# Block products added onto sums in PSUM, the last weight sum made by accumulating transfers, and down rows taken in steps of two

## The chip, the cores and the metric

One Trainium2 chip, one of its cores. The metric is the device time of one execution in microseconds, as the median over several runs. The profile is one profiled execution of the same program; its page gives the span from the first to the last instruction.

## The reference, cut to what matters

Two layers, each of a SwiGLU block, a token mixer (short gated convolution, a gated linear recurrence, a pooling branch), a cross attention and a second SwiGLU block. Each of these four parts ends in a residual sum and a layer norm. Tokens are 256, the model width is 1024, the hidden width of a SwiGLU block is 2816, all in float32. The change touches the four SwiGLU blocks:

```
def swiglu(x, w_gate, w_up, w_down):
    return (jax.nn.silu(x @ w_gate) * (x @ w_up)) @ w_down
h = layer_norm(ALPHA * h + 0.5 * swiglu(h, ffn1_gate[l], ffn1_up[l], ffn1_down[l]), ...)
```

## The kernel before

**Numbers in two parts.** Each float32 operand is split into a rounded high part and the rest: `split` (L60) has ScalarE write the high part (L61) and VectorE subtract it (L62). `mm_rows` (L129) makes one product as three matmuls: high times high, high times low, low times high. `load` (L64) fetches weights through SyncE's queue into a ring of six `raw` tiles of 128x1024, and every one of them is split into a tile `whi` and a tile `wlo`, from rings of eight.

**A SwiGLU block** (`ffn`, L400) walks over the hidden width in chunks of 512, numbered c = 0 to 5, the last of 256. `first` makes chunk 0, `hidden` (L538) the ordinary chunks: all products of x with the gate columns into two PSUM banks (one for each half of the tokens), `activate` (L434) takes them through Silu into the tile `sg`, then all products with the up columns, `gated` (L438) multiplies, and `turn` (L446) brings the result into the layout that the down projection needs: four transfers deal `sg` over the partitions (L450), VectorE transposes 32x32 blocks (L453), and `split` makes `ah` and `al`. `both(c, u)` is one slab of the down projection: 24 matmuls that add chunk c's activations times 256 rows of down into the four `dn` banks (`ys`). Behind the products of chunk c stand `both(c-2, 1)` and `both(c-1, 0)`.

**Block-product chunks.** For c in `sevens` (L679: 2 and 4, in the first block of layer 0 only 4, so seven chunks in all) `by_seven` (L568) computes both gate and up of the chunk with seven products of half the depth (512) and one half of the tokens in place of eight. Blocks of weights (`w00`, `w10` of gate, `w01`, `w11` of up) lie in two tiles each and are summed in place by VectorE (`parts_of`, L593, the add is L597); the sums of blocks of x (`bx`) are made once for a SwiGLU block (`blocks_of_x`, L552) and kept in `kTh` and `kTl`. One product is `run` (L610): 4 depths times 3 matmuls, 12 in all. The seven results go to seven PSUM tiles, four and then three from a ring of four, and are put together by a ScalarE copy (L625) and seven VectorE additions (`put`, L618); `left` (L641) ends with two Silu (L648), two multiplications (L649) and `turn`.

**What sets the order.** The program is written in the order that the text shows, and a scheduling layer places the instructions of each engine; in a few stretches (the start, the recurrence) the order is given by hand. Each engine then runs its own list in order: an instruction that waits holds all that stand behind it on that engine. An instruction that writes into a ring's tile waits until the last reader of the tile before it is done.

**PSUM layout.** `product` (L102) writes column c + 256 h of the result to place 2c + h of the bank. `by_two` (L430) therefore reads a bank in two instructions, one for each parity, with 256 elements each.

Of the kernel before, what the change touches and what calls it, by code (L numbers as in the profile page):

```python
# [17 lines left out]
P = 128  # L18
# [28 lines left out]
def model(ctx: ExitStack, tc: tile.TileContext, t: dict, out: bass.AP):  # L47
# [13 lines left out]
        nc.scalar.copy(hi, src)  # L61
        lows.append(nc.vector.tensor_tensor(lo, src, hi.bitcast(F32), op=ALU.subtract))  # L62

    def load(src, k0, nk, c0, ncol, fine=False):  # L64


        hi, lo, todo = [], [], []
        step = 2048 // ncol
        for a in range(k0, k0 + nk, step):
            half = step // 2  # L70
            raw = [
                wp.tile([P, 1024], F32, tag="raw", name="raw", bufs=6).rearrange("p (k c) -> p k c", c=ncol)
                for _ in range(2)
            ]
            part = 1 if fine else half
            for b in range(0, step, part):
                loads.append(nc.sync.dma_start(
                    raw[b // half][:, b % half : b % half + part, :],
                    src[(a + b) * P : (a + b + part) * P, c0 : c0 + ncol].rearrange("(k p) c -> p k c", p=P),
                ))  # L80
# [12 lines left out]
        return Weights(hi, lo, half, todo)  # L93
# [5 lines left out]
            "p (h c) -> p h c" if len(a.shape) == 2 else "p r (h c) -> p r h c", h=2  # L99
        )  # L100

    def product(o, w, x, start, stop):  # L102
        x = x.rearrange("p (h c) -> p c h" if len(x.shape) == 2 else "p r (h c) -> p r c h", h=2)
        o = o.rearrange("p (c h) -> p c h" if len(o.shape) == 2 else "p r (c h) -> p r c h", h=2)
        nc.tensor.matmul(o, w, x, start=start, stop=stop)  # L105


    def sums(o):
# [17 lines left out]
        nc.vector.tensor_tensor(dst, o[:, 0], dst, op=ALU.add)  # L126


    def mm_rows(o, xh, xl, wh, wl, start, stop):  # L129
        product(o, xh, wh, start, False)  # L130
        product(o, xh, wl, False, False)
        product(o, xl, wh, False, stop)

    def tok(i):
        return slice(i * P, (i + 1) * P)
# [47 lines left out]
    def load_memory(mp, behind):  # L183
        m = [
            mp.tile([P, DM], F32, tag=f"spare{n}", name="m", bufs=1).rearrange("p (k b j) -> p k b j", k=4, j=32)
            for n in range(2)
        ]
        with tc.issue_after(behind.ins):
            for n in range(2):
                for a in range(4):  # L190
                    for k in range(4):
                        c = (4 * n + k) * P + a * 32
                        nc.gpsimd.dma_start(
                            m[n][a * 32 : a * 32 + 32, k],
                            t["mem"][0, :, c : c + 32].rearrange("(b i) j -> i b j", i=32),
                        )

        def later():
            for n in range(2):
                for k in range(0, 4, 2):  # L200
                    turned = mp.tile([P, 2, SEQ], F32, tag="up", name="turned")
                    nc.vector.transpose(
                        turned.rearrange("p k t -> p (k t)"), m[n][:, k : k + 2].rearrange("p k b j -> p (k b j)")
                    )
                    d = slice(4 * n + k, 4 * n + k + 2)
                    split(mTh[:, d, :], mTl[:, d, :], turned)

        return later

# [190 lines left out]
    def ffn(l, name, n, pend=None, last=False, early=None):  # L400
        gate, up, down = (t[f"{name}_{x}"][l] for x in ("gate", "up", "down"))
        with tc.tile_pool(name="ffn", bufs=2, reuse_waits="tile") as fp:
# [22 lines left out]


            def ordered(v):
                return v.rearrange("p (a k j) -> p k a j", a=4, j=32)

            def by_two(v, o):  # L430
                o = o.rearrange("p (n a j m) -> p m n a j", n=2, a=4, m=2)
                return [(ordered(v)[:, 2 * m : 2 * m + 2], o[:, m]) for m in range(2)]

            def activate(s, i, og):  # L434
                for v, o in by_two(s[:, i, :], og):
                    nc.scalar.activation(v, o, AF.Silu)

            def gated(s, i, ou):  # L438
                for v, o in by_two(s[:, i, :], ou):
                    nc.vector.tensor_tensor(v, o, v, op=ALU.mult)  # L440

# [4 lines left out]
            def turn(s):  # L446
                ah, al = act_tiles()
                x = fp.tile([P, 4, NT, P], F32, tag="dealt", name="dealt", bufs=1)
                for a in range(4):
                    nc.sync.dma_start(x[a * 32 : a * 32 + 32], s[:, :, a * P : (a + 1) * P])  # L450
                for i in range(NT):
                    d = fp.tile([P, 4, P], F32, tag="up", name="square")
                    nc.vector.transpose(  # L453
                        d.rearrange("p k (b r) -> p b k r", b=4), x[:, :, i, :].rearrange("p b (k j) -> p b k j", k=4)
                    )
                    split(ah[:, :, tok(i)], al[:, :, tok(i)], d)
                return ah, al

            def first():
# [105 lines left out]
                    split(*parts[n], q[o])  # L565
                return parts

            def by_seven(c0, bx):  # L568
                def rows_by_columns(r):
                    return r.rearrange("p (k c) -> p k c", c=CHUNK)  # L570

# [38 lines left out]
                def run(o, x, w):  # L610
                    for k in range(4):
                        wh, wl = w.at(k, slice(0, CHUNK))
                        mm_rows(o, x[0][:, k, :], x[1][:, k, :], wh, wl, k == 0, k == 3)

                def half_sum():
                    return fp.tile([P, 4, P], F32, tag="up", name="half").rearrange("p k t -> p (k t)")

                def put(o, a, op, b):  # L618
                    nc.vector.tensor_tensor(halves(o), sums(a), halves(b), op=op)

                s = activations()
                g = [s[:, i, :] for i in range(NT)]
                o = [acc((P, CHUNK)) for _ in range(4)]
                run(o[0], part_of_x(0, 0), parts_of(w00))
                nc.scalar.copy(halves(g[0]), sums(o[0]))  # L625
                run(o[2], bx[0], parts_of(w00, w01))
                run(o[1], bx[1], parts_of(w00, w11))
                e = half_sum()
                put(e, o[1], ALU.add, g[0])
                run(o[3], bx[2], parts_of(w01, w11))  # L630
                put(g[1], o[3], ALU.add, e)
                f = half_sum()
                put(f, o[2], ALU.subtract, g[1])
                put(e, o[2], ALU.subtract, e)
                o = [acc((P, CHUNK)) for _ in range(3)]
                run(o[0], bx[3], parts_of(w11))
                run(o[1], part_of_x(0, 1), parts_of(w10))
                run(o[2], part_of_x(1, 1), parts_of(w00, w10))


                def left():  # L641
                    put(e, o[0], ALU.add, e)
                    for i in range(NT):
                        put(g[i], o[1 + i], ALU.add, g[i])
                    s = fp.tile([P, NT, CHUNK], F32, tag="spare2", name="sg", bufs=1)
                    for i, u in enumerate((e, f)):
                        v = ordered(s[:, i, :])
                        nc.scalar.activation(v, g[i].rearrange("p (k a j) -> p k a j", a=4, j=32), AF.Silu)  # L648
                        nc.vector.tensor_tensor(v, v, u.rearrange("p (k a j) -> p k a j", a=4, j=32), op=ALU.mult)  # L649
                    return turn(s)  # L650

                return left
# [1 line left out]
            def last_hidden(c0):  # L654

                ah, al = act_tiles()
                s = activations()[:, 0, :].rearrange("p (j c) -> p j c", j=2)
                r = fp.tile([P, 2, SEQ], F32, tag="up", name="up")
# [12 lines left out]
                return ah, al  # L671

            def slab(c, u):
                w = load(down, c * 4 + 2 * u, 2, 0, DM)
                ah, al = acts[c]
                return w, ah[:, 2 * u : 2 * u + 2, :], al[:, 2 * u : 2 * u + 2, :]

# [34 lines left out]
            for c, (c0, ncol) in enumerate(chunks):  # L712
# [1 line left out]
                    acts.append(first())  # L714
                    ys = [[acc((P, 512), "dn") for _ in range(2)] for _ in range(NT)]
                elif c in sevens:
                    left = by_seven(c0, bx)
                else:
                    if c in (1, 2) and early is not None:
                        acts.append(hidden(c0, aside))  # L720
# [500 lines left out]
```

## Time and profile before

| what | value |
|---|---|
| median of 3 runs | 1071.56 us (1070.53 to 1072.04) |
| span of the profiled execution | 1068.8 us |
| TensorE busy, granted clock | 1059.3 us, 0.998 |
| VectorE busy | 946.3 us (89%) |
| ScalarE busy | 642.4 us (60%) |
| GpSimd busy | 66.4 us (6%) |
| DMA moved | 231.90 MB |

The page gives the span of the profiled execution (its own time within the kernel); the runs' times contain 2 to 3 us around it. "Busy" of TensorE is modelled: matmuls overlap, one begins before the one ahead has ended, so the distance from start to start is what counts. In rows of instruction groups the columns are line, engine, operation, output<-inputs, count | total us, mean ns of one | idle time just before them and what ended it. In rows of the timeline they are start, duration, engine, line, operation, tiles and count, and in brackets the idle time ahead and what ended it.

### The profile page before, as it was taken

Reading aid. Unit: us, or ns where it says so; the run is one execution under the profiler, and the core shown is the slowest. Engines: PE = TensorE matmul, PEld = TensorE weight load, DVE = VectorE, ACT = ScalarE, POOL = GpSimd, SP = SyncE. Lnnn points to the kernel's source line nnn. Section 1 sums busy time; section 2 is a strip of 40 time slices with the busy share of each in tenths; the row PEclk is TensorE's granted clock in tenths of the full one; section 3 lists DMA queues with packets and bytes.
Section 4 is the critical chain, followed back from the end, with each engine's and each line's share of the span. In section 5 each row is a group of like instructions: output and inputs, shape, how many; then the busy total and the mean of one; then the engine's idle time right before and its main releaser. Section 6 shows DMA issues by size and latency. Waiting matters only on the chain.

```text
span 1068.8 us, 16312 instructions
## 1 busy us (share of the span) xinstructions
PE 1059.3 (99%) x5966; PEld 937.7 (88%) x5966; DVE 946.3 (89%) x1318; ACT 642.4 (60%) x916; POOL 66.4 (6%) x114
## 2 busy tenths in 40 slices
PE   9999999999999999999999999999999999999997
PEld 7888888889899888888888888888898998888886
DVE  6977997998988799999799999788989787999996
ACT  7555664666557565656575557566764665656660
POOL 9700001000000000000000000010000000000000
PEclk9999999999999999999999999999999999999999
DMA  9997484755574575848675865856536665759461
GB/s 362 262 307 256 129 288 165 249 176 174 170 278 167 178 252 194 290 167 218 238 272 184 256 254 183 290 179 216 196 126 213 241 227 181 257 156 334 134 223 40
DMA packets 130895, 231.90 MB, mean 217 GB/s; under 512 B 9408, under 2 KB 48608, under 8 KB 130816
## 3 DMA queue, kind: packets, MB, share of 16 engines
q1 hardware_dynamic: 129024, 228.49, 64.8%
q0 software_dynamic: 1216, 1.20, 0.5%
q8 instruction: 47, 0.77, 0.3%
q10 hardware_dynamic: 576, 1.18, 0.3%
q14 instruction: 32, 0.26, 0.1%
HBM read 216.15 MB, written 1.05 MB: 203 GB/s over the span
## 4 chain that ended last, share of the span: by engine, by line
PE 99%; DMA 0%; DVE 0%; issue 0%; DVEq 0%
PE acc L105 65%; PE dn L105 31%; PE acc L172 1%; PE dn L923 1%; PE dn L982 0%; DMA h<-in_x_dram 0%; PE acc L491 0%; PE dn L981 0%; PE dn L971 0%; PE acc L1047 0%; PE dn L888 0%; DVE h L358 0%; DVE h L353 0%; PE dn L472 0%; DVE st L338 0%
## 5 line engine op out<-in xcount | busy, mean ns | idle before, releaser
L61 ACT CAST whi<-raw 128x1024 fp32r<-128x1024 f32 (+1 forms) x438 | 442.9, 1042 | 197.5 <-DVE raw L597 54.9
L62 DVE TENSOR_TENSOR wlo<-raw,whi 128x1024 fp32r<-128x1024 f32 (+1 forms) x438 | 515.7, 1209 | 32.6 <-ACT whi L61 29.0
L105 PE MATMUL acc<-whi,xT 128*128 128x512 f32 x1032 | 312.9, 380 | 0.0
L105 PEld LDWEIGHTS acc<-whi,xT 128*128 128x128 f32 x1032 | 195.1, 189 | 27.5
L105 PE MATMUL acc<-wlo,xT 128*128 128x512 f32 x516 | 195.6, 379 | 0.0
L105 PE MATMUL acc<-xT,whi 128*128 128x512 f32 x576 | 142.3, 383 | 0.2
L105 PE MATMUL dn<-whi,ah 128*128 128x512 f32 x346 | 131.5, 380 | 0.0
L105 PE MATMUL dn<-wlo,ah 128*128 128x512 f32 x346 | 131.2, 379 | 0.0
L105 PE MATMUL dn<-whi,al 128*128 128x512 f32 x346 | 131.2, 379 | 0.0
L105 PEld LDWEIGHTS acc<-xT,whi 128*128 128x128 f32 x576 | 104.0, 190 | 12.5 <-ACT whi L61 0.7
L105 PEld LDWEIGHTS acc<-wlo,xT 128*128 128x128 f32 x516 | 97.5, 189 | 13.8
L105 PE MATMUL dn<-whi,xT 128*128 128x512 f32 x288 | 87.9, 381 | 0.0
L105 PEld LDWEIGHTS acc<-xT,wlo 128*128 128x128 f32 x576 | 75.5, 191 | 3.9
L105 PE MATMUL acc<-xT,wlo 128*128 128x256 f32 x576 | 75.9, 275 | 0.0
L105 PEld LDWEIGHTS dn<-whi,al 128*128 128x128 f32 x346 | 65.4, 189 | 9.2
L105 PEld LDWEIGHTS dn<-wlo,ah 128*128 128x128 f32 x346 | 65.4, 189 | 9.2
L105 PEld LDWEIGHTS dn<-whi,ah 128*128 128x128 f32 x346 | 65.4, 189 | 9.1
L350 POOL TENSOR_TENSOR rs<-rs,nhalf 128x1 f32<-128x1 f32 x16 | 14.9, 930 | 833.6 <-DVE rs L346 598.1
L597 DVE TENSOR_TENSOR raw<-raw 128x1024 f32<-128x1024 f32 x56 | 66.2, 1217 | 0.4
L105 PEld LDWEIGHTS dn<-whi,xT 128*128 128x128 f32 x288 | 54.4, 189 | 7.7 <-DVE xT L62 0.3
L105 PE MATMUL dn<-wlo,xT 128*128 128x512 f32 x144 | 54.6, 379 | 0.0
L332 DVE SCALAR_TENSOR_TENSOR h<-h,dn 128x512 f32<-128x512 f32 x31 | 21.2, 683 | 32.9 <-PE dn L105 32.9
(234 smaller groups left out, 1277.5 us busy)
## 6 DMA issues: line engine op xcount, KB each, us to landing
raw<-in_ffn_up_dram SPq DMA_DIRECT2D x88, 512.0 KB, 5.3
raw<-in_ffn_down_dram SPq DMA_DIRECT2D x88, 512.0 KB, 6.6
raw<-in_ffn_gate_dram SPq DMA_DIRECT2D x84, 512.0 KB, 5.1
raw<-in_w_in_dram SPq DMA_DIRECT2D x48, 512.0 KB, 4.7
dealt<-sg SPq DMA_DIRECT2D x80, 128.0 KB, 4.7
raw<-in_ca_k_dram SPq DMA_DIRECT2D x16, 512.0 KB, 4.9
raw<-in_w_out_dram SPq DMA_DIRECT2D x16, 512.0 KB, 4.5
raw<-in_ca_v_dram SPq DMA_DIRECT2D x16, 512.0 KB, 5.3
```

The source lines that it names most:

```text
L61: nc.scalar.copy(hi, src)
L62: lows.append(nc.vector.tensor_tensor(lo, src, hi.bitcast(F32), op=ALU.subtract))
L105: nc.tensor.matmul(o, w, x, start=start, stop=stop)
L172: nc.tensor.transpose(pt[:, k, :], src[:, (4 * j + k) * P : (4 * j + k + 1) * P], unit)
L332: nc.vector.scalar_tensor_tensor(v, v, ALPHA / scale, sums(y[i][n]), op0=ALU.mult, op1=ALU.add, accum_out=None if junk is None else st[:, ...
L350: nc.gpsimd.tensor_tensor(rs, rs, nhalf[:, 0:1], op=ALU.pow)
L597: nc.vector.tensor_tensor(r[i], r[i], plus[i], op=ALU.add)
L923: nc.tensor.matmul(o[g, hh, :], kc[:, hh, g], x, start=True, stop=True)
```

## The change

1. **Three products onto closed sums** (`by_seven`). There are three PSUM tiles in place of seven, here A (`o[0]`), B (`o[1]`), C (`o[2]`). In the order of the text: P1 = x00·w00 into A; ScalarE copies A to `s[:,0]` (the s-copy); P2 = bx0·(w00+w01) into B; P3 = bx1·(w00+w11) added onto A; ScalarE copies A to `e` (the e-copy); P4 = x01·w10 into C; P5 = bx2·(w01+w11) added onto A; VectorE adds C to `s[:,0]`, ScalarE takes Silu of it and copies A to `f` (the f-copy); `both(c-2, 1)`; VectorE makes `f` = B - `f`; P6 = bx3·w11 added onto B; P7 = x11·(the last sum of w00) added onto A. Then `both(c-1, 0)` and `left`: Silu of A into `s[:,1]`, `e` = B - `e`, one multiplication of 128x1024, `turn`. TensorE must wait with P3 for the s-copy, with P5 for the e-copy, with P6 for `f`, with P7 for the f-copy.
2. **The last weight sum** is not made by VectorE from `w10`: two DMAs of 512 KB issued by GpSimd add the block of gate from HBM onto the two tiles of `w00` (`accum_op`), after VectorE has made the low parts of (w00+w11).
3. **Down rows in steps of two.** `load(..., dealt=True)` for the slabs of chunks 0 to 4 takes rows 2p + u in place of p; number of DMAs and bytes are the same (each row is 4 KB). The activations then lie in the bank's own order, and `activate` and `gated` read a bank with one instruction of 512 elements in place of two of 256 (`in_order`).
4. **One split in `turn`**: both halves of the tokens are transposed into one tile, and split by one ScalarE and one VectorE instruction of 128x1024 in place of two of 128x512 each. The tag `up` holds one buffer of 4 KB a partition in place of two of 2 KB; the transposed tiles, `e` and `f`, and `turned` of the memory's loading take turns in it.

The core of the diff:

```diff
-    def product(o, w, x, start, stop):
+    def product(o, w, x, start, stop, more=False):
...
-        nc.tensor.matmul(o, w, x, start=start, stop=stop)
+        nc.tensor.matmul(o, w, x, start=start, stop=stop, skip_group_check=more)
...
+                if dealt:
+                    c, u = divmod(a // 2, 2)
+                    at = slice(c * CHUNK + 2 * P * b, c * CHUNK + 2 * P * (b + 1))
+                    rows = src[at, c0 : c0 + ncol].rearrange("(p u) c -> p u c", u=2)[:, u, :]
+                    loads.append(nc.sync.dma_start(to[:, 0, :], rows))
...
             def activate(s, i, og):
-                for v, o in by_two(s[:, i, :], og):
-                    nc.scalar.activation(v, o, AF.Silu)
+                nc.scalar.activation(ordered(s[:, i, :]), in_order(og), AF.Silu)
...
+                d = fp.tile([P, NT, 4, P], F32, tag="up", name="square", bufs=1)
                 for i in range(NT):
-                    d = fp.tile([P, 4, P], F32, tag="up", name="square")
                     nc.vector.transpose(
...
-                    split(ah[:, :, tok(i)], al[:, :, tok(i)], d)
+                d = d.rearrange("p i k t -> p k i t")
+                split(*(y.rearrange("p k (i t) -> p k i t", i=NT) for y in (ah, al)), d)
...
-                o = [acc((P, CHUNK)) for _ in range(4)]
+                ef = fp.tile([P, NT, CHUNK], F32, tag="up", name="halves", bufs=1)
+                e, f = ef[:, 0, :], ef[:, 1, :]
+                def taken(o, bank):
+                    nc.scalar.copy(ordered(o), in_order(bank))
+                o = [acc((P, CHUNK)) for _ in range(2)]
                 run(o[0], part_of_x(0, 0), parts_of(w00))
-                nc.scalar.copy(halves(g[0]), sums(o[0]))
-                run(o[2], bx[0], parts_of(w00, w01))
-                run(o[1], bx[1], parts_of(w00, w11))
...
+                taken(s[:, 0, :], o[0])
+                run(o[1], bx[0], parts_of(w00, w01))
+                run(o[0], bx[1], parts_of(w00, w11), True)
+                for i in range(2):
+                    k = 4 + 2 * i
+                    nc.gpsimd.dma_start(
+                        w00[i], gate[k * P : (k + 2) * P, c0 : c0 + CHUNK].rearrange("(k p) c -> p k c", p=P),
+                        accum_op=ALU.add,
+                    )
+                taken(e, o[0])
+                o.append(acc((P, CHUNK)))
+                run(o[2], part_of_x(0, 1), parts_of(w10))
+                run(o[0], bx[2], parts_of(w01, w11), True)
+                put(s[:, 0, :], o[2], ALU.add, s[:, 0, :])
+                nc.scalar.activation(s[:, 0, :], s[:, 0, :], AF.Silu)
+                taken(f, o[0])
+                between()
+                put(f, o[1], ALU.subtract, f)
+                run(o[1], bx[3], parts_of(w11), True)
+                run(o[0], part_of_x(1, 1), parts_of(w00), True)
...
                 def left():
+                    activate(s, 1, o[0])
+                    put(e, o[1], ALU.subtract, e)
+                    nc.vector.tensor_tensor(s, s, ef, op=ALU.mult)
                     return turn(s)
...
-                    if c > 1:
+                    if c > 1 and c not in sevens:
                         both(c - 2, 1)
+                    if c < len(chunks) - 1:
+                        both(c - 1, 0)
                     if c in sevens:
                         acts.append(left())
-                    if c < len(chunks) - 1:
-                        both(c - 1, 0)
```

`between` is `both(c-2, 1)`; `run` with `more` true starts no new sum. The number of matmuls is the same.

More of the change, by code (lines that the diff above doesn't have):

```diff
@@ L62, in split, with load @@
         lows.append(nc.vector.tensor_tensor(lo, src, hi.bitcast(F32), op=ALU.subtract))
-    def load(src, k0, nk, c0, ncol, fine=False):
+    def load(src, k0, nk, c0, ncol, fine=False, dealt=False):
         hi, lo, todo = [], [], []
@@ L76, in load @@
             for b in range(0, step, part):
[L77 to L80, printed above, removed]
+                to = raw[b // half][:, b % half : b % half + part, :]
+                if dealt:
[3 more added lines that the diff above has]
+                    loads.append(nc.sync.dma_start(to[:, 0, :], rows))
+                else:
+                    loads.append(nc.sync.dma_start(
+                        to, src[(a + b) * P : (a + b + part) * P, c0 : c0 + ncol].rearrange("(k p) c -> p k c", p=P)
+                    ))
             for s in range(2):
@@ L126, in add, with mm_rows @@
         nc.vector.tensor_tensor(dst, o[:, 0], dst, op=ALU.add)
[L129 to L132, printed above, removed]
+    def mm_rows(o, xh, xl, wh, wl, start, stop, more=False):
+        product(o, xh, wh, start, False, more)
+        product(o, xh, wl, False, False, more)
+        product(o, xl, wh, False, stop, more)
     def tok(i):
@@ L200, in later @@
                 for k in range(0, 4, 2):
-                    turned = mp.tile([P, 2, SEQ], F32, tag="up", name="turned")
+                    turned = mp.tile([P, NT, CHUNK], F32, tag="up", name="turned", bufs=1)[:, 0, :]
                     nc.vector.transpose(
-                        turned.rearrange("p k t -> p (k t)"), m[n][:, k : k + 2].rearrange("p k b j -> p (k b j)")
+                        turned, m[n][:, k : k + 2].rearrange("p k b j -> p (k b j)")
                     )
                     d = slice(4 * n + k, 4 * n + k + 2)
-                    split(mTh[:, d, :], mTl[:, d, :], turned)
+                    split(mTh[:, d, :], mTl[:, d, :], turned.rearrange("p (k t) -> p k t", k=2))
         return later
@@ L427, in ordered, with in_order @@
             def ordered(v):
[L428 to L432, printed above, removed]
+                return v.rearrange("p (a k j) -> p a k j", a=4, j=32)
+            def in_order(o):
+                return o.rearrange("p (a j k) -> p a k j", a=4, j=32)
             def activate(s, i, og):
-                for v, o in by_two(s[:, i, :], og):
-                    nc.scalar.activation(v, o, AF.Silu)
+                nc.scalar.activation(ordered(s[:, i, :]), in_order(og), AF.Silu)
             def gated(s, i, ou):
-                for v, o in by_two(s[:, i, :], ou):
-                    nc.vector.tensor_tensor(v, o, v, op=ALU.mult)
+                v = ordered(s[:, i, :])
+                nc.vector.tensor_tensor(v, in_order(ou), v, op=ALU.mult)
             def turn(s):
@@ L450, in turn @@
                     nc.sync.dma_start(x[a * 32 : a * 32 + 32], s[:, :, a * P : (a + 1) * P])
+                d = fp.tile([P, NT, 4, P], F32, tag="up", name="square", bufs=1)
                 for i in range(NT):
-                    d = fp.tile([P, 4, P], F32, tag="up", name="square")
                     nc.vector.transpose(
-                        d.rearrange("p k (b r) -> p b k r", b=4), x[:, :, i, :].rearrange("p b (k j) -> p b k j", k=4)
-                    )
-                    split(ah[:, :, tok(i)], al[:, :, tok(i)], d)
+                        d[:, i].rearrange("p k (b r) -> p b k r", b=4),
+                        x[:, :, i, :].rearrange("p b (k j) -> p b k j", k=4),
+                    )
+                d = d.rearrange("p i k t -> p k i t")
+                split(*(y.rearrange("p k (i t) -> p k i t", i=NT) for y in (ah, al)), d)
                 return ah, al
@@ L566, in blocks_of_x, with by_seven @@
                 return parts
-            def by_seven(c0, bx):
+            def by_seven(c0, bx, between):
                 def rows_by_columns(r):
@@ L608, in part_of_x, with run @@
                     return xTh[:, d, tok(i)], xTl[:, d, tok(i)]
-                def run(o, x, w):
+                def run(o, x, w, more=False):
                     for k in range(4):
                         wh, wl = w.at(k, slice(0, CHUNK))
-                        mm_rows(o, x[0][:, k, :], x[1][:, k, :], wh, wl, k == 0, k == 3)
-                def half_sum():
-                    return fp.tile([P, 4, P], F32, tag="up", name="half").rearrange("p k t -> p (k t)")
+                        mm_rows(o, x[0][:, k, :], x[1][:, k, :], wh, wl, k == 0 and not more, k == 3, more)
@@ L618, in put @@
                 def put(o, a, op, b):
-                    nc.vector.tensor_tensor(halves(o), sums(a), halves(b), op=op)
+                    nc.vector.tensor_tensor(ordered(o), in_order(a), ordered(b), op=op)
                 s = activations()
-                g = [s[:, i, :] for i in range(NT)]
-                o = [acc((P, CHUNK)) for _ in range(4)]
-                run(o[0], part_of_x(0, 0), parts_of(w00))
-                nc.scalar.copy(halves(g[0]), sums(o[0]))
-                run(o[2], bx[0], parts_of(w00, w01))
@@ L627, in by_seven @@
-                run(o[1], bx[1], parts_of(w00, w11))
[L628 to L637, printed above, removed]
@@ L638, in by_seven @@
-                run(o[2], part_of_x(1, 1), parts_of(w00, w10))
-                def left():
[L642 to L649, printed above, removed]
+                ef = fp.tile([P, NT, CHUNK], F32, tag="up", name="halves", bufs=1)
@@ L657, in last_hidden @@
                 s = activations()[:, 0, :].rearrange("p (j c) -> p j c", j=2)
-                r = fp.tile([P, 2, SEQ], F32, tag="up", name="up")
+                r = fp.tile([P, NT, CHUNK], F32, tag="up", name="up", bufs=1)[:, 0, :].rearrange("p (j c) -> p j c", j=2)
                 for m, o in ((gate, s), (up, r)):
@@ L673, in slab @@
             def slab(c, u):
-                w = load(down, c * 4 + 2 * u, 2, 0, DM)
+                w = load(down, c * 4 + 2 * u, 2, 0, DM, dealt=c < len(chunks) - 1)
                 ah, al = acts[c]
@@ L716, in ffn @@
                 elif c in sevens:
-                    left = by_seven(c0, bx)
+                    left = by_seven(c0, bx, lambda: both(c - 2, 1))
                 else:
```

## The prediction

> **What bounds the kernel now.** I read the head of the page first, then the answer on TensorE's own waits, then the chain in order of time at the chunks that change.
>
> ```profile
> span 1068.8 us, 16312 instructions
> ...
> PE 99%; DMA 0%; DVE 0%; issue 0%; DVEq 0%
> ```
>
> ```profile
> PE dn L472 <- DVE kTh L467: 1.5, 1, 1.5
> PE acc L491 <- DMA h<-in_x_dram: 0.5, 1, 0.5
> ```
>
> ```profile
> 410.62 5.18 PE dn L105 x24
> 415.80 18.13 PE acc L105 x84
> 433.93 10.36 PE dn L105 x48
> 444.29 20.72 PE acc L105 x96
> 465.01 10.36 PE dn L105 x48
> ```
>
> The chain is TensorE's own stream, and TensorE waits for another engine only 2.0 us, both at the start. A block-product chunk is 84 matmuls in 18.13 us, 0.216 us each; a down slab of 24 takes 5.18, also 0.216; the ordinary chunk's 96 take 20.72, again 0.216. So these chunks run at one rate, without a gap. One product of 12 matmuls is 2.59 us.
>
> ```profile
> 415.80:444.29 28.49, 28.49 (x134) 24.91 (x133) 28.49 (x32) 18.28 (x22) 0.00 (x0) 1.00 0.75 216
> 444.29:475.37 31.08, 31.08 (x146) 27.23 (x145) 29.10 (x31) 17.06 (x21) 0.00 (x0) 1.00 0.68 248
> 475.37:503.86 28.49, 28.49 (x134) 24.96 (x133) 28.49 (x32) 20.09 (x22) 0.00 (x0) 1.00 0.68 197
> ```
>
> Columns: sum, TensorE, its weight loads, VectorE, ScalarE, GpSimd, granted clock, DMA share, GB/s. In the first and third row (chunks 2 and 4) VectorE is busy for the whole 28.49 us, as TensorE is; the clock is 1.00. VectorE is full and yet costs nothing: the ring of eight split tiles keeps TensorE fed. Taking work from VectorE therefore cannot shorten this program. Only a new wait of TensorE can move the time, and upward.
>
> **The change part by part.**
>
> *Instructions saved.*
>
> ```profile
> L62 DVE TENSOR_TENSOR wlo<-raw,whi 128x1024 fp32r<-128x1024 f32 (+1 forms) x438 | 515.7, 1209 | 32.6 <-ACT whi L61 29.0 <-PE acc L105 1.9
> L597 DVE TENSOR_TENSOR raw<-raw 128x1024 f32<-128x1024 f32 x56 | 66.2, 1217 | 0.4
> L453 DVE STREAM_TRANSPOSE square<-dealt 128x512 f32<-128x512 f32 x40 | 26.0, 687 | 9.0 <-DMA dealt<-sg 7.8 <-issue 1.2
> L619 DVE TENSOR_TENSOR half<-acc,sg 128x512 f32<-128x512 f32 x14 | 9.6, 684 | 0.0
> ```
>
> In each of seven block chunks VectorE loses two weight additions (2 x 1.22) and four of the seven `put` (4 x 0.68), 5.2 us; the single split and the single multiplication save some tenths more. Some 37 us of VectorE's time over the program, 0 us of the path, since no wait of TensorE on VectorE stands in the chunks. The same holds for `activate` and `gated` in one instruction. The down rows in steps of two are the same count of DMAs and bytes; I cost them at 0, covered by the ring of `raw` tiles. ScalarE gains two copies of about 0.58 in a block chunk, within its 8 to 10 us of idle time there.
>
> *Matmuls.* Their number and shapes are the same; in the built order TensorE still has 84 and 48 of them in a block chunk. 0 us.
>
> *New waits.* P3, P5, P6 and P7 add onto a bank that ScalarE or VectorE must have read. What matters is what stands ahead of those copies in ScalarE's list. I lay the built order of the changed kernel over the durations of before, for chunk 2 (415.80) and chunk 4 (475.37). T is the start of P1.
>
> **Chunk 2, three times in the program.** TensorE's order there is P1, P2, two matmuls of P4, P3, the other ten of P4, two of `both`, P5, 22 of `both`, P6, P7. So P3 is due at T+5.18+0.43 = T+5.61 = 421.41, and P5 at 421.41 + 24 x 0.216 = 426.59.
>
> ```profile
> 398.83 1.23 DVE L62 TENSOR_TENSOR wlo<-raw,whi 128x1024 fp32r<-128x1024 f32 x1 [1.05 <-ACT whi L61]
> ...
> 410.98 1.22 DVE L62 TENSOR_TENSOR wlo<-raw,whi 128x1024 fp32r<-128x1024 f32 x1
> ...
> 416.18 5.76 DVE L62 TENSOR_TENSOR wlo<-raw,whi 128x1024 fp32r<-128x1024 f32 x5
> 421.86 1.30 DVE L453 STREAM_TRANSPOSE square<-dealt 128x512 f32<-128x512 f32 x2
> ```
>
> ```profile
> 414.10 4.13 ACT L61 CAST whi<-raw 128x1024 fp32r<-128x1024 f32 x4 [4.82 <-DVE raw L597]
> 418.47 1.06 ACT L61 CAST whi<-raw 128x1024 fp32r<-128x1024 f32 x1 [0.24 <-PE acc L105]
> 419.78 1.05 ACT L61 CAST whi<-raw 128x1024 fp32r<-128x1024 f32 x1 [0.25 <-PE acc L105]
> 420.73 0.58 ACT L625 COPY sg<-acc 128x512 f32<-128x512 f32 x1
> ...
> 422.59 1.21 ACT L61 CAST ah<-square 128x512 fp32r<-128x512 f32 x2 [0.34 <-DVE square L453]
> ...
> 430.18 6.74 ACT L61 CAST whi<-raw 128x1024 fp32r<-128x1024 f32 x7 [5.42 <-DVE raw L597]
> ```
>
> The s-copy: the cast at 418.47 is set free by the end of P1 (415.80+2.59 = 418.39), so a release costs 0.08; the cast at 419.78 by half of P2. The new order has the s-copy behind that cast as before, so it ends at 420.73+0.58 = 421.31, and P3 is due at 421.41. About 0.
>
> The e-copy: ScalarE's new list from the s-copy on is one cast, the split of the activations (`ah`, which needs both transposes), three casts, of which the third reads the accumulated `w00`, and then the e-copy. So P5 hangs on VectorE's transposes. VectorE at 398.83 had been idle, so its start there is the same. From there its new order is: low part of w00, addition, two transposes, addition, low part, low part of the activations, low part, three additions, a `gated`, a low part, a `gated`, and the last low part that reads the first half of w00. With 1.15 for each of the eleven 1024-wide ones (5.76 over 5), 1.23 for the two transposes and 0.60 for each `gated` (L619's 684 ns less the overlap), that is 12.65+1.23+1.2, so 413.9. Then the second half's addition, to 415.05; its cast on ScalarE, about 1.05, leaves VectorE idle to 416.15; five low parts, to 421.9; the transposes, to 423.15. Before they ended at 421.86+1.30 = 423.16: what VectorE saves, and one addition moved ahead, cancel up to here. ScalarE then: `ah` 423.2 to 424.2, casts at 0.95 from start to start (6.74 for seven), the third begun at 426.05, the e-copy 427.0 to 427.6. P5 is due at 426.59 and begins at about 427.7: **1.1 us lost**. Before, the same three casts were late as well, but nothing of TensorE hung on them. In the order behind it P6 is 4.75 us of `both` further on; `f` is ready by 432.4 and P6 due at 435: nothing more.
>
> **Chunk 4, four times.** The list is kinder: ahead of the s-copy stand casts that TensorE has freed by T+1.3, and the `ah` split.
>
> ```profile
> 473.74 2.35 DVE L597 TENSOR_TENSOR raw<-raw 128x1024 f32<-128x1024 f32 x2
> 476.01 1.30 DVE L453 STREAM_TRANSPOSE square<-dealt 128x512 f32<-128x512 f32 x2
> ```
>
> The two additions in the first row are those that go, so the transposes come at 473.7 and `ah` 2.3 us earlier. The s-copy then ends by T+3.4 (P3 due at T+5.18), the e-copy follows P3's end at T+7.8 and ends by T+8.6 (P5 due at T+10.36), `f` by T+15.3 (P6 due at T+18.1). 0 us.
>
> *The accumulating DMAs.* No row shows one. The first is issued when its half of w00 is free, at 413.9 in chunk 2, and its cast's turn is at 426.05: 12 us of cover. In chunk 4 about the same, and 3.5 us more before `f` is late.
>
> ```profile
> raw<-in_ffn_down_dram SPq DMA_DIRECT2D x88, 512.0 KB, 6.6
> ...
> lng<-in_ln_g_dram SPq DMA_DIRECT2D x8, 512.0 KB, 3.7
> ...
> m<-in_mem_dram POOLq DMA_DIRECT2D x32, 32.0 KB, 5.8
> ```
>
> Transfers of the same size land in 3.7 to 6.6 us, GpSimd's own of 32 KB in 5.8. I bound the accumulating one by 3.7 below and 2 x 6.6 = 13.2 above (a second read of the same size), and take 7, by the row of 6.6: hidden. At 13.2 it is not.
>
> The Trainium skill has a rule that speaks against this part. Its page "Collectives: The Full Stack", section "The bandwidth ceiling: the fold count and why AG ≠ RS ≠ AR", says that an addition in the DMA path halves the rate because it needs two source reads (62.28 against 32.35 GB/s measured there). No run here shows it yet; by it the upper bound is the right end, and rival B is what it would do.
>
> **Sum.** Three chunks with 1.1 us and the wake of TensorE, some 3.4 us in all, onto the profiled span: 1068.8 to 1072.2. The median stands 2.8 over that span, so 1071.56 + 3.4 = **1075.0 us**. A measurement of this kernel tells about 0.2%, 2.1 us, from no change.
>
> **The rivals.**
> - *A, not slower:* ScalarE reaches the e-copy of chunk 2 in time. One mechanism decides it, the end of the two transposes: at 422.0 in place of 423.15 the e-copy ends before 426.59. For it speaks that VectorE is the engine relieved, and that four low parts ahead of them could come early; against it, that my sum reproduces 423.16. Up to 0.7 us per chunk the time stays within 2.1 us: 1071.6, chance 0.30.
> - *B, the accumulating transfer is late:* at 13.2 us plus 0.7 for its issue it lands at T+12.0; cast and e-copy follow to T+13.5, P5 begins at T+13.6 in place of T+10.79: 2.8 us in each chunk 2. In chunk 4 `f` comes at T+17.4, just in time. 1071.6 + 8.5 = 1080.1, chance 0.15. For it speaks that DMA share is 0.75 in the chunk; against it 12 us of cover.
> - *C, faster:* VectorE's relief shows on the path. TensorE's waits are 2.0 us, all at the start, which is unchanged, so 1069.5 at most; chance 0.05.
>
> **How the numbers follow.** The forecast, 0.5 to 2 us in each of three chunks, has 0.50; A 0.30, B 0.15, C 0.05. Slower by over 0.2%: 0.50 + 0.15 = 0.65. Within: 0.30. Faster: 0.05. The range reaches down over A, to 1071.0, and up to B's 1080.5.
>
> **What would show it.** In the profile after: a gap of about 1 us ahead of P5 in chunk 2, put down to ScalarE's copy at the new L633, and none in chunk 4; VectorE with idle time in the block chunks; additions of weights x42 in place of x56; the DMAs from GpSimd landing within 12 us. The forecast is wrong if chunk 2 keeps 18.13 us for 84 matmuls (A), or if ScalarE waits for the DMA ahead of the e-copy (B), or if a gap stands somewhere that I took as covered: the start of layer 0, where `turned` shares the single `up` buffer, or the s-copy, with only 0.1 us of slack.

## The result and the profile after

The changed kernel takes 1075.03 us (median of 5 runs, 1074.71 to 1075.69) against 1071.56 (5 runs): ratio 1.0034, 95% interval 1.0022 to 1.0047, so 3.5 us slower. The profiled execution took 1074.71 us, its span is 1072.9, 4.1 over that of before.

The head of the page and two of its groups, changed kernel:

```profile
span 1072.9 us, 16246 instructions
PE 1060.8 (99%) x5966; PEld 937.3 (87%) x5966; DVE 913.3 (85%) x1223; ACT 647.0 (60%) x884; POOL 83.1 (8%) x128
...
L604 DVE TENSOR_TENSOR raw<-raw 128x1024 f32<-128x1024 f32 x42 | 50.0, 1216 | 0.5
```

VectorE is 33.0 us less busy (946.3 to 913.3), the weight additions are x42 in place of x56, and the program is slower: the relieved engine was not on the path. TensorE's own waits show what is new (columns: what waited, for what, total us, times, longest):

```profile
PE acc L112 <- ACT halves L633: 1.8, 3, 0.7
PE dn L479 <- DVE kTh L474: 1.5, 1, 1.5
PE acc L112 <- ACT sg L633: 0.5, 2, 0.3
PE acc L498 <- DMA h<-in_x_dram: 0.5, 1, 0.5
```

The two rows with L633 are new: three times for the e-copy (`halves`), and, shorter, for the s-copy (`sg`). Three is the number of chunks 2 that are made as block products. The same window that was full before, and chunk 4's:

```profile
415.60:444.09 28.49, 27.68 (x127) 23.63 (x126) 27.18 (x26) 21.93 (x25) 1.19 (x1) 1.00 1.03 337
...
476.67:505.16 28.49, 28.49 (x134) 24.95 (x133) 25.00 (x24) 21.58 (x24) 0.00 (x0) 1.00 0.95 279
```

TensorE is no longer busy throughout chunk 2, but still is in chunk 4; VectorE now has idle time in both (28.49 before; 27.18 and 25.00 now). TensorE's timeline at the two places in the first chunk 2:

```profile
420.99 0.38 PE L112 MATMUL acc<-wlo,xT 128*128 128x512 f32 x1
421.68 0.48 PE L112 MATMUL acc<-whi,kTh 128*128 128x512 f32 x1 [0.32 <-ACT sg L633]
422.00 0.38 PE L112 MATMUL acc<-wlo,kTh 128*128 128x512 f32 x1
...
426.75 0.38 PE L112 MATMUL dn<-wlo,ah 128*128 128x512 f32 x1
427.63 0.48 PE L112 MATMUL acc<-whi,kTh 128*128 128x512 f32 x1 [0.50 <-ACT halves L633]
427.95 0.38 PE L112 MATMUL acc<-wlo,kTh 128*128 128x512 f32 x1
```

Read starts, not brackets: the bracket counts from the modelled end of the matmul ahead, and so leaves out part of the gap. From start to start a matmul takes 0.216. Ahead of P3 it is 421.68 - 420.99 = 0.69, so 0.48 lost; ahead of P5 it is 0.88, so 0.66 lost; and the first matmul after each wait takes 0.32, so 0.10 more for filling again. The other two chunks 2:

```profile
589.97 0.38 PE L112 MATMUL acc<-wlo,xT 128*128 128x512 f32 x1
590.52 0.48 PE L112 MATMUL acc<-whi,kTh 128*128 128x512 f32 x1 [0.17 <-ACT sg L633]
...
595.59 0.38 PE L112 MATMUL dn<-wlo,ah 128*128 128x512 f32 x1
596.61 0.48 PE L112 MATMUL acc<-whi,kTh 128*128 128x512 f32 x1 [0.64 <-ACT halves L633]
```

```profile
949.97 0.38 PE L112 MATMUL acc<-wlo,xT 128*128 128x512 f32 x1
950.49 0.48 PE L112 MATMUL acc<-whi,kTh 128*128 128x512 f32 x1
...
955.56 0.38 PE L112 MATMUL dn<-wlo,ah 128*128 128x512 f32 x1
956.61 0.48 PE L112 MATMUL acc<-whi,kTh 128*128 128x512 f32 x1 [0.68 <-ACT halves L633]
```

By the same reckoning 0.34 and 0.80, 0.30 and 0.84. In all three chunks the two gaps add up to 1.14. Three times 1.14 and six refills of 0.10 are 4.0 us, nearly the whole of the 4.1.

### The profile page after: what moved, and what is told of

Same layout as the page of the kernel before. It is cut to its first block, busy times and chain, and to the rows that moved or that the text cites. A ratio compares the mean times of both kernels' runs of the same rounds, so it can differ in the third digit from the quotient of the medians.

```text
span 1072.9 us, 16246 instructions
## 1 busy us (share of the span) xinstructions
PE 1060.8 (99%) x5966; PEld 937.3 (87%) x5966; DVE 913.3 (85%) x1223; ACT 647.0 (60%) x884; POOL 83.1 (8%) x128
## 3 DMA queue, kind: packets, MB, share of 16 engines
HBM read 223.49 MB, written 1.05 MB: 209 GB/s over the span
## 4 chain that ended last, share of the span: by engine, by line
PE 92%; DVE 3%; DMA 1%; issue 1%; ACT 1%; SPq 0%; DVEq 0%; ACTq 0%
PE acc L112 60%; PE dn L112 29%; DVE wlo L62 1%; PE acc L179 1%; DMA dealt<-sg 1%; ACT whi L61 1%; PE dn L936 1%; SPq L455 0%; PE dn L995 0%; DVE raw L604 0%; DMA h<-in_x_dram 0%; DVE h L365 0%; PE acc L498 0%; DVE sg L445 0%; DVE h L360 0%
## 5 line engine op out<-in xcount | busy, mean ns | idle before, releaser
L604 DVE TENSOR_TENSOR raw<-raw 128x1024 f32<-128x1024 f32 x42 | 50.0, 1216 | 0.5
```

Source lines behind the costliest of these rows:

```text
L604: nc.vector.tensor_tensor(r[i], r[i], plus[i], op=ALU.add)
```

## Experiments

Theory Q: the loss is ScalarE's queue in chunk 2, where the s-copy and the e-copy stand behind casts of weights. Rivals: D, the accumulating transfers cost it (the prediction's rival B is one form of it); B, from here on, a product that adds onto a bank which was just read costs TensorE time by itself. Kernels are edits of the changed kernel unless said otherwise; each is compared with runs of the kernel before beside it (median 1070.8 to 1071.0).

### e2: the last sum by VectorE again

```diff
-                    nc.gpsimd.dma_start(
-                        w00[i], gate[k * P : (k + 2) * P, c0 : c0 + CHUNK].rearrange("(k p) c -> p k c", p=P),
-                        accum_op=ALU.add,
-                    )
...
-                run(o[0], part_of_x(1, 1), parts_of(w00), True)
+                run(o[0], part_of_x(1, 1), parts_of(w00, w10), True)
```

> The accumulating transfers are gone; VectorE adds w10 onto w00 as in the kernel before, two additions more in a block chunk, everything else as in the kernel after. Theory Q (the loss is ScalarE's queue in chunk 2: the e-copy and the s-copy stand behind casts there): the extra addition falls into VectorE's 1.2 us of idle time ahead of the transposes, the queue is as before, so the gaps ahead of P3 (0.3 to 0.5 us) and P5 (0.7 to 0.8 us) stay and the time is 1075.0 us, 0.7 either way. Rival D (the transfers cost it, by landing late or by contention): gaps gone, 1071.6. Rival B (a product that adds onto a bank which was just read costs TensorE time by itself): 1075.0.

Measured: 1074.89 us, ratio 1.0040 (1.0028 to 1.0053). The waits:

```profile
PE acc L112 <- ACT halves L633: 2.3, 3, 0.8
PE dn L479 <- DVE kTh L474: 1.5, 1, 1.5
```

D falls as the cause of the loss: without a transfer it is the same. How it divides over the two waits differs: by starts, 0.22 ahead of P3 and 0.92 ahead of P5 in each chunk, again 1.14. The e-copy's lateness is the loss; a late P3 only takes its share of it beforehand.

### e3: the turned activations split in two halves again

```diff
-                split(*(y.rearrange("p k (i t) -> p k i t", i=NT) for y in (ah, al)), d)
+                for i in range(NT):
+                    split(ah[:, :, tok(i)], al[:, :, tok(i)], d[:, i])
```

> The split of the turned activations is made in two halves again, each behind its own transpose; nothing else differs from the kernel after. In the built order of chunk 2 the e-copy then stands behind two casts of weights in place of three, and P5 directly behind P4. Theory Q: the e-copy ends about 0.95 us earlier, near 426.7, P5 is due at 426.5, so its gap shrinks from 0.7 to 0.8 us to about 0.2; the gap ahead of P3 stays. 1075.0 less 3 x 0.6 to 0.8: 1072.9 us (1072.4 to 1073.4). Rival D as contention and rival B: 1075.0.

Measured: 1072.52 us, ratio 1.0017 (1.0008 to 1.0026). ScalarE's timeline:

```profile
421.79 0.59 ACT L633 COPY sg<-acc 128x512 f32<-128x512 f32 x1 [0.24 <-DMA dealt<-sg]
422.27 1.05 ACT L61 CAST whi<-raw 128x1024 fp32r<-128x1024 f32 x1
423.26 1.22 ACT L61 CAST ah<-square 128x512 fp32r<-128x512 f32 x2
424.38 2.04 ACT L61 CAST whi<-raw 128x1024 fp32r<-128x1024 f32 x2
426.33 0.58 ACT L633 COPY halves<-acc 128x512 f32<-128x512 f32 x1
```

Two casts stand between `ah` and the e-copy in place of three, and P5 loses nothing; P3's gaps (0.65, 0.30, 0.62) are left. The e-copy starts 1.25 us earlier against P1 than in the changed kernel (10.16 behind it, 11.41 there). 0.95 of this is the cast that no longer stands ahead of it; for the rest, the first half of `ah` no longer waits for the second transpose. Half of the loss is given back (ratio 1.0034 to 1.0017): Q. In the two chunks with the longer gaps ahead of P3, the s-copy itself sat idle for a dealing transfer (0.24 us in the row above, 0.22 in the third chunk), so a part of what is left is not the queue of casts. The run doesn't say that the single split is wrong in itself; its price came by way of the scheduler's order.

### e4: seven banks, nothing added on

```diff
-                run(o[0], bx[1], parts_of(w00, w11), True)
+                run(o[2], bx[1], parts_of(w00, w11))
...
-                taken(e, o[0])
+                put(e, o[2], ALU.add, g[0])
-                run(o[0], bx[2], parts_of(w01, w11), True)
+                run(o[4], bx[2], parts_of(w01, w11))
+                put(g[1], o[4], ALU.add, e)
...
-                run(o[1], bx[3], parts_of(w11), True)
-                run(o[0], part_of_x(1, 1), parts_of(w00), True)
+                run(o[1], part_of_x(1, 1), parts_of(w00))
+                run(o[0], bx[3], parts_of(w11))
```

> No product adds onto an earlier one's bank: each of the seven has its own, and VectorE makes the sums as in the kernel before (six puts); accumulating transfers, the single split and the rows in steps of two stay; P7 runs ahead of P6. Theory Q: no wait on the copies is left; VectorE's puts free P6's bank near 434, ahead of its need at 436; 1071.6 us (1071.0 to 1072.3), no gap of over 0.2 us in chunk 2. Rival D: 1075.0. Rival B: 1071.6 too.

Measured: 1071.11 us, ratio 1.0003 (0.9994 to 1.0012). Its waits are those of before:

```profile
PE dn L479 <- DVE kTh L474: 1.5, 1, 1.5
PE acc L498 <- DMA h<-in_x_dram: 0.4, 1, 0.4
```

So the transfers, the single split and the rows in steps of two together cost and bring nothing that can be measured without the additions onto PSUM; the loss comes with these and the copies that they wait for.

### e5: the same additions, with work between copy and product

```diff
-                run(o[0], bx[1], parts_of(w00, w11), True)
+                third = parts_of(w00, w11)
...
-                taken(e, o[0])
                 o.append(acc((P, CHUNK)))
                 run(o[2], part_of_x(0, 1), parts_of(w10))
+                run(o[0], bx[1], third, True)
+                taken(e, o[0])
+                between(0)
                 run(o[0], bx[2], parts_of(w01, w11), True)
...
-                between()
+                between(1)
```

`between(i)` is the slab's 12 matmuls of one half of the tokens.

> All of the kernel after, but TensorE's order in a block chunk is P1, P2, P4, P3, half of the old down slab, P5, the other half, P6, P7, so that 12 matmuls (2.59 us) lie between a copy's source and the product that adds onto its bank. Theory Q: P3 is due at T+7.8 and the s-copy ends near T+6.5, P5 is due at T+13.0 and the e-copy ends near T+12.5, so all six gaps are gone: 1071.3 us (1070.8 to 1072.0). Rival D: 1075.0, as the transfers are the same. Rival B: 1075.0, as the banks added onto are the same.

Measured: 1071.36 us, ratio 1.0006 (0.9998 to 1.0015). ScalarE's copies come later than in the changed kernel, and no matmul waits for one:

```profile
421.64 0.59 ACT L633 COPY sg<-acc 128x512 f32<-128x512 f32 x1 [0.32 <-DMA dealt<-sg]
...
428.15 0.57 ACT L633 COPY halves<-acc 128x512 f32<-128x512 f32 x1
```

There is little to spare: the e-copy ends at 428.7, and P5 begins at 428.97, on time. B falls, since the same four products add onto the same banks (P3, P5 and P7 onto A, P6 onto B; the first point of the change counts three). The price was the distance, not the addition.

### e11 and e12: VectorE's work ahead of the queue, more and less

In e11 VectorE makes `ah`; in e12 w01 + w11 is made by transfers too.

```diff
-                split(*(y.rearrange("p k (i t) -> p k i t", i=NT) for y in (ah, al)), d)
+                hi, lo = (y.rearrange("p k (i t) -> p k i t", i=NT) for y in (ah, al))
+                nc.vector.tensor_copy(hi, d)
+                lows.append(nc.vector.tensor_tensor(lo, d, hi.bitcast(F32), op=ALU.subtract))
```

```diff
+                for i in range(2):
+                    k = 4 + 2 * i
+                    nc.gpsimd.dma_start(
+                        w01[i], up[k * P : (k + 2) * P, c0 : c0 + CHUNK].rearrange("(k p) c -> p k c", p=P),
+                        accum_op=ALU.add,
+                    )
...
-                run(o[0], bx[2], parts_of(w01, w11), True)
+                run(o[0], bx[2], parts_of(w01), True)
```

> The copy of the turned activations (ah) is made by VectorE in place of ScalarE, so that ScalarE's queue in chunk 2 no longer waits for the transposes; VectorE has one copy of about 1.15 us more in each turn, one of them ahead of the last weight addition that frees ScalarE's six casts. Built order: P3 directly behind P2. Theory Q whole (what counts is the queue of casts ahead of the copies, and that begins with VectorE's addition): the casts start 1.15 us later, near 416.3, the s-copy ends near 422.7, P3 waits 1.5 to 2 us, the e-copy follows near 428, total loss 2 to 2.4 us in each of three chunks: 1077 to 1079 us. Theory Q as the prediction put it (the e-copy hangs on the transposes by way of ah): the e-copy comes in time, only P3's gap is left, 1072.5 to 1073.5.

> The kernel after with one more sum by transfers: w01 + w11 is made by two accumulating transfers as well, so that VectorE has two additions fewer ahead of chunk 2. Built order: P3 directly behind P2, P5 directly behind P4, the e-copy one cast earlier. Theory Q whole: VectorE's last weight addition and the six casts come 1 to 2 us earlier; the s-copy still stands behind casts whose tiles P1 and P2 must free and ends near 421.2, P3 is due at 420.8; the e-copy is about in time: 0.5 to 0.8 us lost in each of three chunks, 1072.5 to 1073.5 us. Rival D (transfers cost it): twice as many of them, slower than the kernel after, 1076 to 1079.

e11 measured 1074.63 us, ratio 1.0035 (1.0021 to 1.0048): outside both expectations. ScalarE there, with P1 at 417.33:

```profile
417.46 4.84 ACT L61 CAST whi<-raw 128x1024 fp32r<-128x1024 f32 x5 [4.69 <-DVE raw L606]
422.21 0.58 ACT L635 COPY sg<-acc 128x512 f32<-128x512 f32 x1
...
428.40 0.58 ACT L635 COPY halves<-acc 128x512 f32<-128x512 f32 x1 [0.32 <-DVE al L465]
```

VectorE's copy (L464, tile view of `ah`; ns min/median/max) was shorter than the 1.15 us that I had counted:

```profile
L464 DVE CAST ah<-square x2: 682/682/683, 405.3 to 425.4; 128x1024 fp32r<-128x1024 f32 x2
```

So the casts moved only by 0.6 us against P1 (from 0.47 ahead of it to 0.13 behind), and P3 lost 0.32. ScalarE's own queue no longer held the e-copy, but it waited for VectorE's low part of the activations (`al`): `halves` and the turned tile share the single `up` buffer, which in the changed kernel is free in time (its low part ends at 426.55, the e-copy begins at 427.00). This second wait hid behind the first. P5 lost 0.48. Together 0.8 and two refills in each of three chunks are 3.0 of the 3.9 us in the medians. The rest isn't placed: in the profiled execution the program's start took longer too.

e12 measured 1071.45 us, ratio 1.0006 (0.9997 to 1.0015): faster than either theory said. Two additions fewer on VectorE, and the casts of chunk 2 begin 2.0 us earlier against P1 (413.82, with P1 at 416.32); P5 never waits. One gap is left, 0.7 us ahead of P3 in the second chunk 2:

```profile
589.19 0.58 ACT L633 COPY sg<-acc 128x512 f32<-128x512 f32 x1 [1.35 <-DMA dealt<-sg]
```

There the s-copy waits until the previous chunk's dealing transfers have read `sg`. So the queue begins with VectorE's weight additions, as Q says in full; but one cast fewer stands ahead of the s-copy here as well (five in place of six), and the two were not separated. More transfers shift the wait to a transfer.

### e6, e6c, e7: a third block chunk, to spend VectorE's relief

```diff
-            sevens = (2, 4) if early is None else (4,)
+            sevens = (2, 3, 4) if early is None else (4,)
```

e6 is this on e5, e6c this on e5 and e12's transfers, e7 this on the kernel before.

> As the kernel with P4 ahead of P3 and half a slab ahead of P5 (e5), and chunk 3 is a block-product chunk too in the three feed-forward blocks that have two already: 3 x 12 matmuls fewer, 3 x 2.59 = 7.8 us of TensorE. By instruction counts VectorE has about 32.7 us of work in a block chunk after the change (14 + 4 low parts and 6 additions of 1.14, three puts of 0.6, transposes, one multiplication, one low part of the activations), 37.4 in one of before, 17.5 in an ordinary one; TensorE has 28.49 in a block chunk. Three block chunks in a row need 98 us of VectorE in 85.5 of TensorE; the lead of eight split tiles covers about 9 of it. Theory Q says that VectorE's relief is worth nothing where it is not spent: here it is spent, 1063.6 us plus what VectorE is late, 0 to 5 us in each of three: 1063.6 to 1075, most likely 1070. Rival V (VectorE is far from binding after the change): 1063.6.

> As e6_spread_three, and the sum w01 + w11 is made by two accumulating transfers too, so that VectorE has two additions fewer in a block chunk: about 30.4 us, 91 in three against 85.5. Theory Q with the lead of the tiles: VectorE is hardly late, 1064 to 1068 us. If the transfers cost by contention (3 MB more over the program's block chunks, DMA share 1.02 in chunk 2 of the kernel after), it is no faster than e6_spread_three.

> The kernel before with chunk 3 as a block-product chunk too in the same three feed-forward blocks, nothing else. VectorE then needs 3 x 37.4 = 112 us in three chunks of 28.49 (85.5): it is late by 26.7 less a lead of about 9 us in each of three blocks, against 7.8 us saved on TensorE. Theory Q: slower than before, 1085 to 1125 us, TensorE's waits put down to VectorE. If VectorE were not what keeps the kernel before from a third block chunk: 1063.8.

Measured: e6 1093.64 us, ratio 1.0209 (1.0195 to 1.0223); e6c 1092.08, 1.0212 (1.0190 to 1.0234); e7 1134.77, 1.0596 (1.0580 to 1.0612). All miss: 12 fewer matmuls in each of three chunks save 7.8 us, and yet the kernels are 21 to 64 us slower. In e6, chunk 3 and chunk 4:

```profile
444.00:475.00 31.00, 27.26 (x118) 22.99 (x117) 29.66 (x29) 19.93 (x23) 2.37 (x2) 0.94 0.82 251
475.00:505.00 30.00, 28.32 (x128) 23.18 (x127) 29.97 (x30) 21.93 (x26) 2.38 (x2) 1.00 0.64 177
```

VectorE is all but full and TensorE waits, and the granted clock falls to 0.94 in chunk 3. The lead of eight tiles that I had counted on did not cover it. In e6c, where VectorE has less to do, ScalarE sits idle ahead of chunk 3 until that chunk's weights land:

```profile
439.91 1.05 ACT L61 CAST whi<-raw 128x1024 fp32r<-128x1024 f32 x1 [5.04 <-DMA raw<-in_ffn_gate_dram]
```

The blocks of gate lie in single tiles (`spare0` to `spare2`), which chunk 2 holds until its last sum; two block chunks in a row cannot load ahead. That this is the limit in e6c was read from the trace and not tried. What the three runs do show: with a third block chunk the change (in e5's order) is worth some 40 us, 1134.8 against 1093.6, and with two it is worth nothing. That it is VectorE which binds there fits its busy time, but the place of the blocks in `spare0` to `spare2` and the lower clock act in e6 and e7 too, and no run takes them apart. No version was found that beats the kernel before.

## Why the prediction was right, point by point

- **VectorE's relief is worth 0** (some 37 us by count): right; 33.0 us less busy, and e4, which keeps the transfers' share of it, takes the same time as before. Activate and gated in one instruction, the single split, rows in steps of two at 0: right together (e4), not tried one by one.
- **The e-copy in chunk 2, 1.1 us each**: right in place and cause; in size in part by chance. ScalarE and VectorE in the changed kernel:

```profile
415.12 5.78 ACT L61 CAST whi<-raw 128x1024 fp32r<-128x1024 f32 x6 [4.69 <-DVE raw L604]
421.05 0.58 ACT L633 COPY sg<-acc 128x512 f32<-128x512 f32 x1 [0.15 <-DMA dealt<-sg]
421.53 1.05 ACT L61 CAST whi<-raw 128x1024 fp32r<-128x1024 f32 x1
423.21 1.05 ACT L61 CAST ah<-square 128x1024 fp32r<-128x1024 f32 x1 [0.63 <-DVE square L458]
424.16 2.94 ACT L61 CAST whi<-raw 128x1024 fp32r<-128x1024 f32 x3
427.00 0.57 ACT L633 COPY halves<-acc 128x512 f32<-128x512 f32 x1
```

```profile
413.79 1.22 DVE L604 TENSOR_TENSOR raw<-raw 128x1024 f32<-128x1024 f32 x1
416.19 5.77 DVE L62 TENSOR_TENSOR wlo<-raw,whi 128x1024 fp32r<-128x1024 f32 x5 [1.19 <-ACT whi L61]
421.88 1.30 DVE L458 STREAM_TRANSPOSE square<-dealt 128x512 f32<-128x512 f32 x2
```

  Forecast: last addition 413.9, transposes to 423.15, `ah` 423.2, e-copy 427.0 to 427.6. Laying the new order over old durations gave ScalarE's and VectorE's times right to 0.1 us. TensorE's were not: P1 starts 0.16 us earlier than the prediction had it (next point), so P5 was due at 426.43 in place of 426.59, and the forecast's own times make 1.27. In the trace P5 starts 1.25 us late, the two gaps of 1.14 and the refill behind the first.
- **The s-copy, about 0**: the step that failed, though it cost little; the prediction had named a gap there as a sign against it. First, the slack of 0.1 us was not there. The prediction took T, 415.80, from the chain, whose piece begins at the modelled end of the matmul ahead (415.42 + 0.38). By starts, in the kernel before, P1 begins at 415.64:

```profile
415.42 0.38 PE L105 MATMUL dn<-whi,al 128*128 128x512 f32 x1
415.64 0.38 PE L105 MATMUL acc<-whi,xT 128*128 128x512 f32 x1
```

  So P3 was due at 421.25, ahead of the forecast end of the s-copy, 421.31. Second, the prediction left out a wait: the s-copy writes into `sg`, which the previous chunk's dealing transfers must have read, and the last of these came late beside an accumulating transfer. From the chain of the changed kernel:

```profile
414.76 6.19 DMA dealt<-sg
```

  It landed at 420.95, and the s-copy ran from 421.05 to 421.63. The casts were hardly later than before: six in a row from 415.12 end at 420.90, against 420.83. In e2, without accumulating transfers, the s-copy follows its casts at once and P3 loses 0.22 in each chunk; the changed kernel's 0.48, 0.34 and 0.30 are 0.26, 0.12 and 0.08 more. What P3 loses, P5 no longer has to wait (e2 and the changed kernel have the same sum); the second wait doubled the refills.
- **The wake**, 0.1 for all: mis-sized, and taken from no row; it is 0.10 after each wait, twice in each chunk, 0.6 in all. 3.4 forecast, 4.0 in the trace, 3.5 in the medians.
- **Chunk 4, no stall**: right (28.49 of 28.49).
- **The transfers, 7 us between 3.7 and 13.2, hidden**: right for their own landing, 7.6 us at most. That they would delay the dealing transfers was not foreseen. The issues of L642, then the groups for GpSimd's and SyncE's transfers of the same size:

```profile
DMA to landing us min/median/max: 5.7/6.6/7.6
```

```profile
raw<-in_ffn_gate_dram SPq DMA_DIRECT2D x84, 512.0 KB, 5.5
...
raw<-in_ffn_gate_dram POOLq DMA_DIRECT2D x14, 512.0 KB, 6.6
```

  The adding transfer takes 6.6 / 5.5 = 1.2 times as long, not twice (the two also differ in the engine that issues them). The Trainium skill states the halved rate ("Collectives: The Full Stack", section "The bandwidth ceiling: the fold count and why AG ≠ RS ≠ AR") for rings of three or more ranks; the prediction carried it over to a single transfer. In one transfer of this size it does not show; the measurement decides.
- **Rivals**: A needed the transposes at 422.0; they ended at 423.2. B needed 13.2 us. C had no wait to remove. For the change's idea the Trainium skill has a sentence ("Perfetto Trace Analysis", section "Matmuls"): "Independent matmul groups should rotate through different PSUM banks so the ACT/DVE evacuation of one overlaps the next group's matmuls". The runs agree (e4, with a tile of its own for each product, against the changed kernel: 1071.1 and 1075.0), and e5 adds that 12 other matmuls in between serve as well as another bank.

## What to carry to other kernels

An addition onto a bank that another engine must read first puts that engine's whole queue on TensorE's path: lay the built order of the queue ahead of the copy over measured durations, starting from the engine that feeds it, and put independent matmuls between copy and addition. Take TensorE's due times from starts in the timeline, not from pieces of the chain, and list what the copy must wait for besides its queue, transfers that read its target too. Where several late copies stand in a chain, their gaps share one lateness; take the last one's, and add a refill for each. Relief for an engine that is full but not awaited is worth nothing by itself.

## What the runs showed that was not expected

- A transfer that deals `sg` was delayed where an accumulating one was issued ahead of it. Of the four ahead of the first chunk 2, the kernel before, then the changed kernel:

```profile
DMA to landing us min/median/max: 2.9/3.1/3.1
```

```profile
DMA to landing us min/median/max: 2.9/3.0/6.2
```

  In the three chunks 2 the last of the four took 5.8 to 6.5 us in the changed kernel, e3, e4 and e5, and 3.1 to 3.2 in the kernel before and e2, which have no accumulating transfer. It took 3.2 in e11 too, which has the same transfers as the changed kernel but issues the first at 416.51, behind the last dealing one (415.97); the changed kernel issues it at 414.17, ahead of that (414.76). The s-copy sat idle 0.15 us for it in the changed kernel's first chunk 2, and 1.35 in e12's second.
- VectorE copied 128x1024 into `ah` in 0.68 us, where its subtraction of the same size takes 1.22 and ScalarE's cast 1.05.
- A matmul that has waited takes 0.32 us to the start of the next in place of 0.216.
